# Two weight matrices of a hybrid block: seven block products for eight in 45 of 128 squares

## The chip, the cores and the metric

The kernel runs on one core of a Trainium2 chip. The time is the device time of one execution in microseconds (us); the median of three runs of the kernel before is 2197.33 us (2196.93 to 2197.67). The profile is of one more execution.

## The reference

One layer, 256 positions, width 4096, all in float32. The input is normalised and multiplied by `w_in`; the columns of the product feed an mLSTM branch (8 heads) and a sparse-attention branch (16 heads), whose outputs stand side by side in `y`. Two square matrices of 4096 by 4096 follow, and they are what the change is about:

```python
x = x + jnp.concatenate([y_ml, y_ns], axis=-1) @ w_out[layer]
x = x + jax.nn.sigmoid(x @ ple_gate[layer]) * (p[layer] @ ple_proj[layer])
```

`p` has 256 columns, `ple_proj` is 256 by 4096.

## The kernel before

Each float32 product is made of three TensorE products in a rounded format (float32r). A number a is split into a high part, which the format holds, and the rest a - high. ScalarE makes the high part of a weight block (`whi`, line 983) and VectorE the rest (`wlo`, line 984). The same is done for the activations, which lie transposed in eight chunks of 512 rows (`sh` and `sl`, four blocks of 128 rows by 256 positions each). A product is sh x whi + sl x whi + sh x wlo, so three matmuls, all into one float32 accumulator in PSUM.

The work is a list of units. A unit is 256 rows by 512 columns of a weight matrix: one transfer of 512 KB on SyncE's queue into a `raw` buffer, one `whi`, one `wlo` (both 128x1024), and 12 matmuls of 128x512: 2 blocks of rows, 2 halves of the 256 positions (t = 0, 1), 3 products each (`mm` in `wide_group`, lines 733 and 735). A group is 16 units, 512 columns by 4096 rows, and owns two PSUM banks, tag mm0 for t = 0 and mm1 for t = 1. Each tag has two buffers, so a group may begin while the group before it is evicted: `start` requires the eviction of the group before last. The other four banks (`side`) serve everything else. There are 30 groups for w_in, then o0 to o7 for w_out, then g0 to g7 for ple_gate, each of these with one more unit of ple_proj.

The order on each engine is written out by the main loop at the end (there is no scheduler). For unit n it issues the split of unit n + LOOK (LOOK is 2), the next load, what the unit requires, its matmuls, and then one step of a queue of generators, which hold the rest of the work: `urgent` first, then `fifo`. A `require(flag)` steps that queue until the flag is set. The split buffers are LOOK + 1 deep, so the copy for a unit waits until TensorE is done with the unit LOOK + 1 places ahead of it.

Three places matter for the change:

- `t_stat` transposes a finished chunk of y (or of the new x) on TensorE into two side banks and then splits it into `sh` and `sl`; transposes run one chunk ahead of the splits. It runs chunk by chunk while the last group of the stage before still uses the older chunks. For y, the chunks c4 to c7 (columns of the mLSTM) are weighted by `hnw` during the split (lines 674 and 675).
- `t_mo` evicts the last groups of w_in (mo0 to mo3) with a sigmoid on ScalarE (line 638).
- `t_x1` adds x to an evicted group of w_out (line 865). `t_out` makes sigmoid, product with ple_proj's banks and sum for a group of ple_gate; for the last group in halves of 256 columns (lines 916 to 918).

Of the kernel before, what the change touches and what calls it, by code (L numbers as in the profile page):

```python
# [37 lines left out]

LOOK = 2
XN = (16, 19, 22, 25)  # L40
RAWB = 5


@with_exitstack
def hymba_block(ctx: ExitStack, tc: tile.TileContext, a, out: bass.AP):
# [342 lines left out]
    def t_nq(flag, g):  # L388
# [265 lines left out]

    def t_stat(chunks, weighted):

        def trans(c, col0, gate, flag):
            src, o = nat[col0 // 1024], col0 % 1024
            pp = [side(2 * (c % 2) + half, [128, 2, 256]) for half in range(2)]
            for i in range(4):  # L660
                for t in range(2):
                    k = o + i * 128
                    nc.tensor.transpose(pp[i // 2][:, i % 2, t * 128:(t + 1) * 128], src[:, t, k:k + 128], idn)  # L663
            return pp

        def split(pp, c, col0, gate, flag):
            new_stat(c)
            for half in range(2):
# [185 lines left out]
    start2 = len(units)  # L854


    def load_x(n):
        held[f"x{n}"] = utile([128, 2, 512])
        nc.gpsimd.dma_start(held[f"x{n}"], a["x"][:, n * 512:(n + 1) * 512].rearrange("(t p) c -> p t c", p=128))

    def t_x1(ps, flag, n):
        if n % 2 == 0:
            nat[n // 2] = wk.tile([128, 2, 1024], F32, tag=f"nat{n // 2}", name=f"x1_{n // 2}")
        for t in range(2):
            nc.vector.tensor_add(nat[n // 2][:, t, (n % 2) * 512:(n % 2) * 512 + 512], ps[t], held[f"x{n}"][:, t])
        done.add(flag)
        if n + 2 < 8:
            load_x(n + 2)
        yield

    def p2_post(n):
        def post(ps, flag):
            add(t_x1(ps, flag, n))
            ch = [(c, c * 512, f"p2_{c}", f"r{c}") for c in range(8)]
            if n == 6:
                add(t_stat(ch[:7], ()))
            if n == 7:
                add(t_stat(ch[7:], ()))
        return post

    for n in range(8):
        wide_group(f"o{n}", a["w_out"][n], "y" if n == 0 else None, p2_post(n), marks="p2_" if n == 7 else None)


    pbox = {}

    def proj_unit(n):
        def mm(hi, lo):
            ps = [side(2 * (n % 2) + t, [128, 512]) for t in range(2)]
            ph, pl = held["ph"], held["pl"]  # L890
            for t in range(2):
                tk = slice(t * 128, (t + 1) * 128)
                for j in range(2):
                    MM(ps[t], ph[:, j, tk], hi[:, j, :], start=(j == 0), stop=False)  # L894
                    MM(ps[t], pl[:, j, tk], hi[:, j, :], start=False, stop=False)  # L895
                    MM(ps[t], ph[:, j, tk], lo[:, j, :], start=False, stop=(j == 1))  # L896
            pbox[n] = ps
        gemm_unit(a["ple_proj"][n], mm, (lambda: require("r7")) if n == 0 else None)
# [12 lines left out]
    def t_out(ps, flag, n):
        u = utile([128, 2, 512])
        if n == 7:
            for t in range(2):
                for c in (slice(0, 256), slice(256, 512)):
                    nc.scalar.activation(u[:, t, c], ps[t][:, c], AF.Sigmoid)
                    nc.vector.tensor_tensor(u[:, t, c], u[:, t, c], pbox[n][t][:, c], op=OP.mult)
                    nc.vector.tensor_add(u[:, t, c], u[:, t, c], nat[3][:, t, 512 + c.start:512 + c.stop])
                nc.sync.dma_start(out[t * 128:(t + 1) * 128, n * 512:(n + 1) * 512], u[:, t])
            done.add(flag)  # L920
# [5 lines left out]
        for t in range(2):
            nc.vector.tensor_tensor(u[:, t], u[:, t], pbox[n][t], op=OP.mult)
            nc.vector.tensor_add(u[:, t], u[:, t], nat[n // 2][:, t, (n % 2) * 512:(n % 2) * 512 + 512])  # L928
            nc.gpsimd.dma_start(out[t * 128:(t + 1) * 128, n * 512:(n + 1) * 512], u[:, t])  # L929
# [9 lines left out]
    def load(n):  # L939
# [11 lines left out]
        if n in XN:  # L951
            j = XN.index(n)
            nat[j] = wk.tile([128, 2, 1024], F32, tag=f"nat{j}", name=f"xn{j}")
            nc.sync.dma_start(nat[j], a["x"][:, j * 1024:(j + 1) * 1024].rearrange("(t p) c -> p t c", p=128))

    def split(n):
        r = raws.pop(n)
        if n == 0:
            hi = wk.tile([128, 2, 512], F32R, tag="whi", name="whi", bufs=LOOK + 1)
            lo = wk.tile([128, 2, 512], F32R, tag="wlo", name="wlo", bufs=LOOK + 1)  # L960
# [4 lines left out]
            splits[n] = (hi, lo)  # L965
            return
        if n < 16:
            split_x(2 * n)
            split_x(2 * n + 1)
        if n - 1 in XN:  # L970
            done.add(f"xn{XN.index(n - 1)}")
        if units[n]["kind"] == "raw":
            splits[n] = (r, None)
            return
        if units[n]["kind"] == "narrow":
# [4 lines left out]
            return  # L980
        hi = wk.tile([128, 2, 512], F32R, tag="whi", name="whi", bufs=LOOK + 1)
        lo = wk.tile([128, 2, 512], F32R, tag="wlo", name="wlo", bufs=LOOK + 1)
        nc.scalar.activation(hi, r, AF.Copy)  # L983
        nc.vector.tensor_sub(lo, r, hi)  # L984
        splits[n] = (hi, lo)

    N = len(units)
    nload = 0
    while nload < RAWB:
        load(nload)  # L990
        nload += 1
# [54 lines left out]

def _layout(i):
# [48 lines left out]
```

## Time and profile before

| | |
|---|---|
| median of three runs | 2197.33 us |
| the profiled execution's own time | 2197.16 us |
| its span | 2195.4 us |
| TensorE busy | 2187.1 us, 10020 matmuls |
| VectorE busy | 1154.6 us, 53% |
| ScalarE busy | 994.0 us, 45% |
| whi and wlo | 743 each, mean 1060 and 1225 ns |
| matmuls of lines 733 and 735 | 3 x 2940 |
| moved by DMA | 422.02 MB, mean 192 GB/s |

The span is the time from the first to the last instruction. A busy TensorE says that a matmul was in flight; since matmuls are pipelined, its pace is read from the starts in a timeline. In the timeline, "x2" means that two neighbouring instructions are merged in one row, and the bracket is the time that the engine stood idle ahead of it and what ended that.

### The profile page before, as it was taken

Reading aid. Unit: us, or ns where it says so; the run is one execution under the profiler, and the core shown is the slowest. Engines: PE = TensorE matmul, PEld = TensorE weight load, DVE = VectorE, ACT = ScalarE, POOL = GpSimd, SP = SyncE. Lnnn points to the kernel's source line nnn. Section 1 sums busy time; section 2 is a strip of 40 time slices with the busy share of each in tenths; the row PEclk is TensorE's granted clock in tenths of the full one; section 3 lists DMA queues with packets and bytes.
Section 4 is the critical chain, followed back from the end, with each engine's and each line's share of the span. In section 5 each row is a group of like instructions: output and inputs, shape, how many; then the busy total and the mean of one; then the engine's idle time right before and its main releaser. Section 6 shows DMA issues by size and latency. Waiting matters only on the chain.

```text
span 2195.4 us, 26113 instructions
## 1 busy us (share of the span) xinstructions
PE 2187.1 (100%) x10020; PEld 1798.6 (82%) x10020; DVE 1154.6 (53%) x1361; ACT 994.0 (45%) x1235; POOL 38.3 (2%) x82
## 2 busy tenths in 40 slices
PE   9999999999999999999999999999999999999998
PEld 7876888888888888888888888888888888888887
DVE  6553554555556555744564455564444455544444
ACT  6543444454545454444444345453333344444443
POOL 1000000000000000000000000000000000000000
PEclk9999999999999999999999999999999999999999
DMA  9667665555555464565566665656666656666664
GB/s 353 207 200 258 191 192 181 182 165 162 169 165 170 152 181 150 181 195 188 176 192 194 195 188 172 215 180 204 202 212 202 194 178 183 210 207 204 202 202 134
DMA packets 118124, 422.02 MB, mean 192 GB/s; under 512 B 13794, under 2 KB 13850, under 8 KB 118000
## 3 DMA queue, kind: packets, MB, share of 16 engines
q1 hardware_dynamic: 113840, 408.47, 58.7%
q0 software_dynamic: 4016, 11.88, 1.9%
q8 instruction: 78, 1.28, 0.2%
q14 instruction: 46, 0.38, 0.0%
q10 hardware_dynamic: 144, 0.02, 0.0%
HBM read 416.08 MB, written 4.23 MB: 191 GB/s over the span
## 4 chain that ended last, share of the span: by engine, by line
PE 100%; DVE 0%; ACT 0%; ACTq 0%; issue 0%
PE mm L733 61%; PE mm L735 30%; PE sd L508 1%; PE sd L843 1%; PE sd L663 1%; PE sd L504 1%; PE sd L495 0%; PE sd L203 0%; PE sd L894 0%; PE sd L895 0%; PE sd L896 0%; PE sd L418 0%; PE sd L462 0%; PE sd L461 0%; PE sd L460 0%; PE sd L90 0%
## 5 line engine op out<-in xcount | busy, mean ns | idle before, releaser
L984 DVE TENSOR_TENSOR wlo<-raw,whi 128x1024 fp32r<-128x1024 f32 x743 | 910.0, 1225 | 978.3 <-ACT whi L983 973.1
L983 ACT ACTIVATE whi<-raw 128x1024 fp32r<-128x1024 f32 x743 | 787.5, 1060 | 1095.7 <-PE mm L733 988.5
L733 PE MATMUL mm<-whi,sh 128*128 128x512 f32 x2940 | 918.2, 393 | 0.0
L733 PE MATMUL mm<-whi,sl 128*128 128x512 f32 x2940 | 906.8, 390 | 0.0
L735 PE MATMUL mm<-wlo,sh 128*128 128x512 f32 x2940 | 905.7, 389 | 0.0
L733 PEld LDWEIGHTS mm<-whi,sl 128*128 128x128 f32 x2940 | 551.8, 188 | 116.6
L735 PEld LDWEIGHTS mm<-wlo,sh 128*128 128x128 f32 x2940 | 551.8, 188 | 116.2
L733 PEld LDWEIGHTS mm<-whi,sh 128*128 128x128 f32 x2940 | 543.3, 188 | 112.8 <-issue 6.7
L508 PE MATMUL sd<-vsw,pt 128*128 128x128 f32 x192 | 29.9, 292 | 0.0
L478 ACT ACTIVATE s<-s,mx 128x128 f32<-128x128 f32 (+1 forms) x64 | 28.2, 442 | 0.4 <-DVE mx L473 0.4
L508 PEld LDWEIGHTS sd<-vsw,pt 128*128 128x128 f32 x192 | 23.8, 190 | 3.9
L488 ACT ACTIVATE s<-s,sm 128x128 f32<-128x128 f32 (+1 forms) x64 | 25.2, 440 | 0.4 <-DVE sm L484 0.3
L547 DVE SCALAR_TENSOR_TENSOR sq<-u,convw_c,sq 128x256 f32<-128x256 f32 x48 | 23.3, 485 | 1.7
L152 ACT ACTIVATE u<-mm,rt 128x512 f32<-128x512 f32 x12 | 8.3, 689 | 25.4 <-PE mm L735 25.4
L473 DVE TENSOR_REDUCE mx<-s 128x2 f32<-128x256 f32 (+1 forms) x32 | 17.7, 553 | 1.1
L471 DVE TENSOR_TENSOR s<-sd,tb 128x256 f32<-128x256 f32 (+1 forms) x32 | 17.7, 553 | 0.0
L500 DVE COPY pt<-sd 128x256 f32<-128x256 f32 (+1 forms) x32 | 17.6, 550 | 0.0
L843 PE MATMUL sd<-raw,xq 128*60 128x256 f32 x128 | 17.3, 391 | 0.0
L154 DVE TENSOR_SCALAR u<-mm,rt 128x512 f32<-128x512 f32 x12 | 9.0, 751 | 14.5 <-PE mm L735 14.5
L407 POOL DMA_DIRECT2D tb<-rext_d x16 | 8.6, 540 | 458.2 <-DVE s L471 426.1
L495 PEld LDWEIGHTS sd<-idn,s 128*128 128x128 f32 x96 | 12.4, 140 | 4.2
L929 POOL DMA_DIRECT2D out_x<-u x14 | 7.6, 546 | 460.2 <-DVE u L928 460.2
(223 smaller groups left out, 710.7 us busy)
## 6 DMA issues: line engine op xcount, KB each, us to landing
raw<-in_w_in SPq DMA_DIRECT2D x479, 512.0 KB, 3.6
raw<-in_w_out SPq DMA_DIRECT2D x128, 512.0 KB, 3.5
raw<-in_ple_gate SPq DMA_DIRECT2D x128, 512.0 KB, 3.7
raw<-in_w SPq DMA_DIRECT2D x16, 512.0 KB, 3.5
u<-in_xt SPq DMA_DIRECT2D x16, 256.0 KB, 7.6
xn<-in_x SPq DMA_DIRECT2D x4, 1024.0 KB, 6.2
u<-in_x POOLq DMA_DIRECT2D x8, 512.0 KB, 4.9
raw<-in_ple_proj SPq DMA_DIRECT2D x8, 512.0 KB, 3.7
```

Of the source, the lines that this page charges most:

```text
L471: nc.vector.tensor_tensor(sb[i], psd[i], bias[:, None, :].to_broadcast([128, 2, n]), op=OP.add)
L478: nc.scalar.activation(sb[i][:, b], sb[i][:, b], AF.Exp, bias=mx[i][:, b:b + 1], accum_out=sums[i][:, b:b + 1])
L488: nc.scalar.activation(sb[i][:, b], sb[i][:, b], AF.Copy, scale=sums[i][:, b:b + 1])
L504: MM(o[t][:, h, :], pct[32 * h:32 * h + NCMP, t, :], vcmp[32 * h:32 * h + NCMP, g, :], start=True, stop=False)
L508: MM(o[t][:, h, :], ptb[i][:, b, s, :], v[:, s, b, g * 128:(g + 1) * 128], start=False, stop=(b == 1 and s == t))
L547: nc.vector.scalar_tensor_tensor(acc[:, h], c[:, h, i:i + 256], w[:, i:i + 1], acc[:, h], op0=OP.mult, op1=OP.add)
L663: nc.tensor.transpose(pp[i // 2][:, i % 2, t * 128:(t + 1) * 128], src[:, t, k:k + 128], idn)
L733: MM(box["ps"][t], s[c][:, k, t * 128:(t + 1) * 128], m[:, j, :], start=st, stop=False)
L735: MM(box["ps"][t], sh[c][:, k, t * 128:(t + 1) * 128], lo[:, j, :], start=False, stop=last)
L843: MM(o[64 * kv:64 * kv + 60], xq[l // 8][:, l % 8, 60 * kv:60 * kv + 60], raw[:, j, 256 * kv:256 * kv + 256], start=(l == 0), stop=(l == 31))
L983: nc.scalar.activation(hi, r, AF.Copy)
L984: nc.vector.tensor_sub(lo, r, hi)
```

## The change

w_out and ple_gate are now worked in eight groups of 1024 columns (0 to 3 are w_out, 4 to 7 ple_gate), in squares: 256 rows by 1024 columns, with the 256 positions, are two by two by two blocks. kp counts the 16 squares of a group. A whole square ("C") is two units of 12 matmuls. A mixed square is computed with seven block products in place of eight (Winograd's form of Strassen's scheme), so 21 matmuls: the weight blocks and the activation blocks are summed first, and the products land in seven accumulators, from which the four results are summed again. A group has four accumulators of its own results (`own[t][j]`, j the half of the columns) and, where it mixes squares, four others (`oth`, which hold three products and one more shared by results); the two sets of four banks change roles from group to group (`bank`).

A mixed square stands in two parts around a whole one: "a", two units with loads (3 and 6 matmuls), then the whole square, then "c", two units without loads (6 and 6), whose weights are sums of the four raw blocks of "a". `PLANS` gives each group's squares.

```diff
-LOOK = 2
+LOOK = 3
-RAWB = 5
+RAWB = 6
+MIXED = (3, 5, 7, 9, 11, 13)
+def _plan(head, mixed, between, tail):
+    p = [("C", k) for k in head]
+    for m, k in zip(mixed, between):
+        p += [("a", m), ("C", k), ("c", m)]
+    return p + [("C", k) for k in tail]
+PROJ = [("p", 0), ("p", 1)]
+PLANS = [
+    _plan((0, 1, 2, 3), (5, 7, 9, 11, 13), (4, 6, 8, 10, 12), (14, 15)),
...
+] + [_plan((0,), (), (), ()) + PROJ + _plan((1,), MIXED, (2, 4, 6, 8, 10, 12), (14, 15))] * 3
...
+    def bank(bset, i, shape):
+        if bset:
+            return side(i, shape)
+        return psp.tile(shape, F32, tag=f"mm{i // 2}", name=f"mm{i // 2}", bufs=2)
```

Group 1 and 2 mix six squares behind two whole ones, group 3 six behind one, group 4 four behind five whole ones and the two units of ple_proj: 5 + 6 + 6 + 6 + 4 + 3 x 6 = 45. `t_stat` makes the summed activation blocks `cb` of a mixed square behind the split:

```diff
+                kp = 2 * c + half
+                if kp in MIXED:
+                    f = stile([128, 4, 128])
...
+                            nc.scalar.activation(f[:, 2 * i:2 * i + 2].rearrange("p a t -> p (a t)"), p[:, i], AF.Copy,
+                                                 scale=hnw[:, k:k + 1])
...
+                    nc.vector.tensor_sub(f[:, 3:0:-2], f[:, 1::-1], f[:, 3:0:-2])
+                    nc.vector.tensor_sub(f[:, 0], f[:, 0], f[:, 3])
+                    nc.vector.tensor_sub(f[:, 2], f[:, 2], f[:, 0])
+                    cb[kp] = mixed_tiles(kp)
+                    nc.scalar.activation(cb[kp][0], f, AF.Copy)
+                    nc.vector.tensor_sub(cb[kp][1], f, cb[kp][0])
```

The units of a mixed square, and what a group requires when it starts:

```diff
+        def start():
+            require("ev_mo2" if g == 0 else f"oth{g - 1}")
+            if g == 0:
+                require("ev_mo3")
+            if g == 4:
+                require("r1")
+            for i, (t, j) in enumerate(((0, 0), (1, 0), (0, 1), (1, 1))):
+                own[t][j].t = bank(bset, i, [128, 512])
...
+            def split2(r):
+                r0 = raw[kp][0]
+                raw[kp].append(r)
+                hl = split_all(r, keep=True)
+
+                nc.vector.tensor_add(r0[:, 1], r0[:, 1], r0[:, 0])
+                nc.vector.tensor_add(r0[:, 0], r0[:, 0], r[:, 0])
+                nc.vector.tensor_add(r[:, 0], r[:, 0], r0[:, 1])
+                nc.vector.tensor_add(r[:, 1], r[:, 1], r[:, 0])
+                return hl
+            def mm1(hi, lo):
+                emit(product(oth[0], blocks(kp)(0, 0), hi[:, 0], lo[:, 0]))
+            def mm2(hi, lo):
+                emit(product(own[0][0], mixed(kp, 2), hi[:, 0], lo[:, 0]))
+                emit(product(own[0][1], blocks(kp)(1, 0), hi[:, 1], lo[:, 1]))
+            unit(w[kp, 0], split1, mm1, kp, True)
+            unit(w[kp, 1], split2, mm2, kp)
...
+            unit(None, lambda _: split_all(raw[kp][0]), mm1)
+            unit(None, lambda _: split_all(raw[kp][1]), mm2, post=post)
```

`t_x1_oth` and `t_out_oth` sum the four `oth` banks into the group's x or into its two output tiles, `t_x1_own` and `t_out_own` then add the `own` banks. In the last group the latter works in halves of 256 columns, one after the other:

```diff
+        if g == 7:
+            for j in range(2):
+                for t in range(2):
+                    for c in (slice(0, 256), slice(256, 512)):
+                        w = us[j][:, t, c]
+                        nc.vector.tensor_add(w, own[t][j].t[:, c], w)
+                        nc.scalar.activation(w, w, AF.Sigmoid)
+                        nc.vector.tensor_tensor(w, w, pj[:, j, t, c], op=OP.mult)
+                        nc.vector.tensor_add(w, w, x1[:, t, 512 - 512 * j + c.start:512 - 512 * j + c.stop])
+                    nc.sync.dma_start(out[t * 128:(t + 1) * 128, 3584 - 512 * j:4096 - 512 * j], us[j][:, t])
```

Besides, a load is issued as soon as fewer than six raw tiles are held, x is loaded 1024 columns at a time, the products of ple_proj are copied out of their banks, the product of the compressed branch stands last among the accumulations of an attention head, and the scratch for software-made descriptors is 4096 bytes.

On VectorE, in the middle of the w_out stage, the list was nothing but wlo, with the additions of x (line 865) at the end of each group:

```order
L865 TENSOR_TENSOR x_0_11356<-mm_11038,u 128x512
L865 TENSOR_TENSOR x_0_11356<-mm_11039,u 128x512
L984 TENSOR_TENSOR wlo<-raw,whi 128x1024 x16
L865 TENSOR_TENSOR x_0_11356<-mm_11367,u 128x512
L865 TENSOR_TENSOR x_0_11356<-mm_11368,u 128x512
```

Now a pattern of a, whole square and c reads so (line 1243 is wlo of the first unit of a, line 1236 every other wlo, lines 1105 to 1108 the sums of raw weights):

```order
L1243 TENSOR_TENSOR wlo<-raw,whi 128x512
L1236 TENSOR_TENSOR wlo<-raw,whi 128x1024
L1105 TENSOR_TENSOR raw<-raw 128x512
L1106 TENSOR_TENSOR raw<-raw 128x512
L1107 TENSOR_TENSOR raw<-raw 128x512
L1108 TENSOR_TENSOR raw<-raw 128x512
L1236 TENSOR_TENSOR wlo<-raw,whi 128x1024 x4
```

The four sums stand between the wlo of a's second unit and the wlo of the whole square's first; the four wlo at the end are the whole square's two and c's two.

On ScalarE, at the end of w_in's last group mo3 (its banks are mm_10617 and mm_10618 before, mm_10625 and mm_10626 now), before:

```order
L983 ACTIVATE whi<-raw 128x1024 x2
L674 ACTIVATE sh_10973<-sd_10907,hnw_c 128x256 x2
L674 ACTIVATE sh_10973<-sd_10908,hnw_c 128x256 x2
L983 ACTIVATE whi<-raw 128x1024
L674 ACTIVATE sh_11001<-sd_10963,hnw_c 128x256 x2
L674 ACTIVATE sh_11001<-sd_10964,hnw_c 128x256 x2
L983 ACTIVATE whi<-raw 128x1024
L638 ACTIVATE u<-mm_10617,rt 128x512
L638 ACTIVATE u<-mm_10618,rt 128x512
```

and now:

```order
L724 ACTIVATE sh_11014<-sd_10939,hnw_c 128x256 x2
L724 ACTIVATE sh_11014<-sd_10940,hnw_c 128x256 x2
L738 ACTIVATE s<-sd_10940,hnw_c 128x256 x2
L746 ACTIVATE cb<-s 128x512
L1235 ACTIVATE whi<-raw 128x1024
L724 ACTIVATE sh_11050<-sd_11004,hnw_c 128x256 x2
L724 ACTIVATE sh_11050<-sd_11005,hnw_c 128x256 x2
L738 ACTIVATE s<-sd_11005,hnw_c 128x256 x2
L746 ACTIVATE cb<-s 128x512
L1235 ACTIVATE whi<-raw 128x1024
L673 ACTIVATE u<-mm_10625,rt 128x512
L673 ACTIVATE u<-mm_10626,rt 128x512
```

Each of the chunks shown (c5 and c6) has three more ScalarE instructions, lines 738 and 746, and line 746 waits for VectorE's differences; the sigmoids of mo3 keep their place behind them. Group o0 took mo2's two banks at its start; group 0 takes both buffers of mm0 and of mm1, so mo3's too.

On VectorE at the end of the program, before (lines 917 and 918 are product and sum):

```order
L917 TENSOR_TENSOR u<-u,sd_15931 128x256
L918 TENSOR_TENSOR u<-u,x_3_13123 128x256
L917 TENSOR_TENSOR u<-u,sd_15931 128x256
L918 TENSOR_TENSOR u<-u,x_3_13123 128x256
L917 TENSOR_TENSOR u<-u,sd_15932 128x256
```

and now (line 996 adds a bank to the piece; ScalarE's sigmoid, line 997, lies between 996 and 998):

```order
L996 TENSOR_TENSOR u<-sd_15998,u 128x256
L998 TENSOR_TENSOR u<-u,pj 128x256
L999 TENSOR_TENSOR u<-u,x_3_13167 128x256
L996 TENSOR_TENSOR u<-sd_15999,u 128x256
L998 TENSOR_TENSOR u<-u,pj 128x256
L999 TENSOR_TENSOR u<-u,x_3_13167 128x256
```

There were four pieces of two instructions; there are eight of three, and the sigmoid now waits for VectorE and VectorE for the sigmoid within each piece.

## Rows read from the trace of the kernel before

**Rows 1.** The page: engines' busy time, and the chain that ended last, by engine.

```profile
PE 2187.1 (100%) x10020; PEld 1798.6 (82%) x10020; DVE 1154.6 (53%) x1361; ACT 994.0 (45%) x1235; POOL 38.3 (2%) x82
...
PE 100%; DVE 0%; ACT 0%; ACTq 0%; issue 0%
```

**Rows 2.** Timeline of TensorE, last group: start us, length us, engine, line, operation.

```profile
2177.44 0.61 PE L733 MATMUL mm<-whi,sh 128*128 128x512 f32 x2
...
2180.16 0.61 PE L733 MATMUL mm<-whi,sh 128*128 128x512 f32 x2
...
2186.96 0.39 PE L722 MATMUL mm<-whi,sh 128*128 128x512 f32 x1
...
2189.45 0.39 PE L722 MATMUL mm<-wlo,sh 128*128 128x512 f32 x1
```

**Rows 3.** Windows, w_out stage: busy us per engine, granted clock, DMA share, GB/s.

```profile
1500.00:1600.00 100.00, 100.00 (x443) 82.81 (x442) 48.63 (x43) 38.96 (x37) 2.17 (x3) 1.00 0.65 209
```

**Rows 4.** Timeline of all engines, one unit in the last group.

```profile
2175.83 1.06 ACT L983 ACTIVATE whi<-raw 128x1024 fp32r<-128x1024 f32 x1 [1.66 <-PE mm L733]
...
2176.08 0.61 PE L733 MATMUL mm<-whi,sh 128*128 128x512 f32 x2
...
2176.92 1.23 DVE L984 TENSOR_TENSOR wlo<-raw,whi 128x1024 fp32r<-128x1024 f32 x1 [1.49 <-ACT whi L983]
```

**Rows 5.** Timeline of VectorE in the ple_gate stage.

```profile
1913.56 1.23 DVE L984 TENSOR_TENSOR wlo<-raw,whi 128x1024 fp32r<-128x1024 f32 x1 [2.69 <-ACT whi L983]
1914.70 0.68 DVE L927 TENSOR_TENSOR u<-u,sd 128x512 f32<-128x512 f32 x1
1915.42 0.69 DVE L928 TENSOR_TENSOR u<-u,x 128x512 f32<-128x512 f32 x1
1916.03 1.22 DVE L984 TENSOR_TENSOR wlo<-raw,whi 128x1024 fp32r<-128x1024 f32 x1
```

**Rows 6.** Groups by form: count, then busy us, mean ns, idle us ahead.

```profile
L680 DVE TENSOR_TENSOR sl<-sd,sh 128x512 fp32r<-128x512 f32 x24 | 15.3, 681 | 0.0
...
L918 DVE TENSOR_TENSOR u<-u,x 128x256 f32<-128x256 f32 x4 | 1.7, 425 | 0.1
...
L964 DVE TENSOR_TENSOR wlo<-raw,whi 128x512 fp32r<-128x512 f32 x2 | 1.4, 692 | 1.4 <-ACT whi L963 1.4
...
L963 ACT ACTIVATE whi<-raw 128x512 fp32r<-128x512 f32 x2 | 1.3, 630 | 1.3 <-DMA raw<-in_w_in 1.3
...
L488 ACT ACTIVATE s<-s,sm 128x256 f32<-128x256 f32 x32 | 14.3, 494 | 0.1
...
L679 ACT ACTIVATE sh<-sd 128x512 fp32r<-128x512 f32 x24 | 12.8, 585 | 0.0
```

**Rows 7.** Timeline of ScalarE around the start of group o0.

```profile
1451.13 0.48 ACT L674 ACTIVATE sh<-sd,hnw_c 128x256 fp32r<-128x256 f32 x1 [0.58 <-DVE sl L675]
...
1451.50 1.05 ACT L983 ACTIVATE whi<-raw 128x1024 fp32r<-128x1024 f32 x1
...
1453.35 1.06 ACT L983 ACTIVATE whi<-raw 128x1024 fp32r<-128x1024 f32 x1 [0.79 <-ACT whi L983]
...
1463.36 1.26 ACT L638 ACTIVATE u<-mm,rt 128x512 f32<-128x512 f32 x2
```

**Rows 8.** Timeline of TensorE, last transposes ahead of group o0.

```profile
1456.28 1.03 PE L663 MATMUL sd<-idn,y 128*128 128x128 f32 x8
1457.07 0.71 PE L733 MATMUL mm<-whi,sh 128*128 128x512 f32 x2
```

**Rows 9.** Timeline of VectorE at the end of the program.

```profile
2189.39 0.42 DVE L918 TENSOR_TENSOR u<-u,x 128x256 f32<-128x256 f32 x1
...
2189.74 0.41 DVE L917 TENSOR_TENSOR u<-u,sd 128x256 f32<-128x256 f32 x1
...
2191.76 0.42 DVE L918 TENSOR_TENSOR u<-u,x 128x256 f32<-128x256 f32 x1
```

**Rows 10.** Windows, behind the last matmul.

```profile
2192.00:2194.00 2.00, 0.00 (x0) 0.00 (x0) 0.19 (x1) 0.00 (x0) 0.00 (x0) 0.57 0.41 159
```

More of the change, by code (lines that the diff above doesn't have):

```diff
@@ L853, in hymba_block @@
                        after=cmp_unit if name == "vw" else None)
[L854 to L898, printed above, removed]
     def t_p():
-        pr = pttile([128, 2, 256])
+        pr = utile([128, 2, 256])
         nc.gpsimd.dma_start(pr, a["p"])
         yield
-        ph = wk.tile([128, 2, 256], F32R, tag="a", name="ph")
-        pl = wk.tile([128, 2, 256], F32R, tag="b", name="pl")
+        ph, pl = (wk.tile([128, 2, 256], F32R, tag="s", name=n, bufs=3) for n in ("ph", "pl"))
         nc.scalar.activation(ph, pr, AF.Copy)
@@ L908, in t_p, with load_x @@
         held["ph"], held["pl"] = ph, pl
+        done.add("p")
         yield
-    def t_out(ps, flag, n):
-        u = utile([128, 2, 512])
-        if n == 7:
-            for t in range(2):
[L915 to L920, printed above, removed]
+    def load_x(g):
+        nat[g] = wk.tile([128, 2, 1024], F32, tag=f"nat{g}", name=f"x1_{g}")
+        nc.gpsimd.dma_start(nat[g], a["x"][:, g * 1024:(g + 1) * 1024].rearrange("(t p) c -> p t c", p=128))
@@ new lines, in t_out_own @@
+    def t_out_own(g, own, us, pj):
+        while f"mix{g}" not in done:
+            yield
+        x1 = nat[g - 4]
+        if g == 7:
+            for j in range(2):
+                for t in range(2):
[6 more added lines that the diff above has]
+                    nc.sync.dma_start(out[t * 128:(t + 1) * 128, 3584 - 512 * j:4096 - 512 * j], us[j][:, t])
+            done.add("own7")
@@ L921, in t_out @@
             return
-        for t in range(2):
-            nc.scalar.activation(u[:, t], ps[t], AF.Sigmoid)
-        done.add(flag)
+        for j in range(2):
+            for t in range(2):
+                nc.vector.tensor_add(us[j][:, t], own[t][j].t, us[j][:, t])
+        done.add(f"own{g}")
         yield
[L926 to L929, printed above, removed]
+        for j in range(2):
+            u = us[j]
+            nc.scalar.activation(u, u, AF.Sigmoid)
+            nc.vector.tensor_tensor(u, u, pj[:, j], op=OP.mult)
@@ L930, in t_out, with emit @@
             yield
-    for n in range(8):
-        wide_group(f"g{n}", a["ple_gate"][n], "r" if n == 0 else None,
-                   lambda ps, flag, n=n: add(t_out(ps, flag, n)), after=lambda u, n=n: proj_unit(n) if u == 7 else None)
+            c0 = 512 - 512 * j
+            nc.vector.tensor_add(u, u, x1[:, :, c0:c0 + 512])
+            nc.gpsimd.dma_start(out[:, (g - 4) * 1024 + c0:(g - 4) * 1024 + c0 + 512].rearrange("(t p) c -> p t c", p=128), u)
+            yield
+    def emit(seq):
+        for acc, s, m in seq:
+            MM(acc.t, s, m, start=acc.i == 0, stop=acc.i == acc.n - 1)
+            acc.i += 1
@@ L937, in hymba_block @@
+    for g in range(4):
+        pair_group(g, a["w_out"][g], "p1_")
+    for g in range(4, 8):
+        pair_group(g, a["ple_gate"][g - 4], "r")
     raws, splits = {}, {}
@@ L979, in split, with load_some @@
             splits[n] = (hl, None)
[L980 to L985, printed above, removed]
-    N = len(units)
[L988 to L991, printed above, removed]
+            held_raw[0] -= 1
+        elif units[n]["kind"] == "pair":
+            splits[n] = units[n]["split"](r)
+        else:
+            splits[n] = split_all(r)
+    N = len(units)
+    loads = deque(n for n in range(N) if units[n]["src"] is not None)
+    def load_some():
+        while loads and held_raw[0] < RAWB:
+            held_raw[0] += 1
+            load(loads.popleft())
+    load_some()
     add(t_rms())
```

251 lines of the change are left out of this document (226 added, 25 removed).

## The prediction

> **What bounds the kernel now.** I read the page's parts on busy time and on the chain of waits first: TensorE is busy for 2187.1 of 2195.4 us, and the chain that ended last is TensorE alone [rows 1]. A busy TensorE is not yet a dense one, so the timeline comes next, for the pace. The twelve matmuls of one unit (256 rows of weights by 512 columns) start at 2177.44 and those of the next at 2180.16: 2.72 us, 0.2267 us per matmul. Where the last unit's rows stand one by one, six matmuls into the same bank and then six into the other, the first starts at 2186.96 and the twelfth at 2189.45: 0.2264 each [rows 2]. So one accumulator alone runs at the same pace. VectorE is busy in 48.63 of 100 us in the w_out stage [rows 3]. In every stage it is TensorE that sets the end; only what follows the last matmul (2189.45 + 0.39 = 2189.84) is bare.
>
> What I need besides is how a unit's weights get ready. ScalarE starts the copy whi 0.25 us before the next unit's first matmul (2175.83, 2176.08), which is when TensorE is done with the high halves of the unit in whose buffer it writes; it takes 1.06 us, and VectorE's wlo starts 0.03 us behind it and takes 1.23 [rows 4]. VectorE starts an operation that needs nothing from the one ahead 0.09 us before that one ends (1913.56 + 1.23 against 1914.70; 0.61 from a 512-wide start to the next, 1915.42 to 1916.03), but one that waits for its forerunner 0.03 us after its end: 0.72 from start to start (1914.70, 1915.42) [rows 5].
>
> **What is removed.** A whole square is 24 matmuls, a mixed one 21. 45 mixed squares drop 135 matmuls of 128x512: 135 x 0.2267 = 30.6 us off TensorE. ple_proj keeps its 96. The loads are as many and as large as before, so SyncE's queue carries the same; POOL's four loads of x are twice as large and half as many, and each is issued a group ahead of its use.
>
> [...] Rows 2 show 226 to 227 ns here, with a weight load ahead of each, and the measurement decides.
>
> **What is added beside other work.** In a mixed square VectorE makes one 512-wide wlo (0.69), three 1024-wide ones and four 512-wide sums: about 0.6 + 3 x 1.14 + 2.8 = 6.8 us at starts 0.09 apart from ends, where a whole square has 2.3 to 2.5. A repeat of the pattern (mixed square a, whole square, mixed square c) is 45 matmuls, 10.2 us, with 9.2 us of VectorE. By throughput it fits; latency is another matter.
>
> **Term 1, the wait in each repeated pattern.** Put 0 at the first matmul behind the whole square's second unit C2. Units c1, c2, a1', a2' follow (6, 6, 3, 6 matmuls), so C1' starts at 21 x 0.2267 = 4.76, and its fifth matmul, the first with wlo, is due at 5.67. With four buffers, a2' writes into C2's: whi at -0.25 to 0.81, wlo at 0.84 [rows 4]; the first sum 1.14 later at 1.98; each of the other three waits for the one ahead: 2.70, 3.42, 4.14; then C1's wlo, queued behind the sums, at 4.14 + 0.61 = 4.75 to 5.98 [rows 5]. TensorE waits 0.31, with a hop 0.35 us. The first pattern of a group has none (its a2 writes into a buffer freed two units earlier): 45 - 8 = 37 waits, 13.0 us. Bounds: 0, were the sums all 0.61 apart (the chain then ends at 5.65, before it is due); 0.55 each (20 us), were every operation held to 0.72. I take 0.35, the rows' own spacing.
>
> [...]
>
> **Term 2, the start of group 0.** Its four accumulators need both buffers of both tags, so its second matmul waits for the sigmoid that evicts mo3's first bank; before, group o0 took only mo2's. On ScalarE that sigmoid stands behind whi's and the splits of chunks c4 to c6. It started at 1463.36 (two in 1.26) [rows 7]; mo3's last matmuls follow the transposes at 1456.28, 24 of them from 1457.07, so TensorE is free at 1462.5 [rows 8]. Even undelayed, the second matmul (due 1462.7) would wait to 1464.0: 1.3 us. Now each of c4, c5, c6 gets, between its fourth sh copy and the next whi (1451.13, 1451.50: nothing lies there now), two more 256-wide copies, three short differences on VectorE, the copy to cb: 0.37 + 0.48 + 0.03 + 0.43 + 2 x (0.03 + 0.29) + 0.03 + 0.63 = 2.6, less the 0.05 of a pipelined start, 2.55 [rows 6, 7] (0.29 for 128 columns is an estimate from 0.692 at 512 and 0.425 at 256). Only one slack lies in that chain, 0.79 before whi at 1453.35, of which VectorE's queue leaves 0.7. Three times 2.55 less 0.7 is 6.95; the wait is 1.3 + 6.95 = 8.2 us. Chunks c1 to c3 come out even: split, sums and two wlo's need 6.3 us of the 6.33 that TensorE gives them. Bounds 6 and 10. Behind the waiting matmul stands all of group 0; ScalarE and VectorE catch up while TensorE waits, so nothing further is late.
>
> [...]
>
> **Term 3, the start of group 4.** Chunk 1 of the new stationary is transposed into the two banks of own[0][1] and own[1][1], so the eighth matmul waits until VectorE has read them. VectorE has ahead of that the four own-adds of group 3 (the third waits for the last unit; 0.61 apart they end 1.85 us behind group 3), one wlo (to 2.97) and two sl of 0.68, to 4.2; due was 1.59 [rows 5, 6]. Wait 2.6. After that each chunk c1 to c6 with its sums holds ScalarE and VectorE for 5.2 us (two sl 1.2, differences 1.0, copy 0.63, whi 1.06, wlo 1.25), while TensorE has 2.72 + 0.79 of work per chunk [rows 2, 8]; weights are three units ahead, and the side banks run out at c6 and c7: another 2.0. Together 4.6, bounds 2 and 8.
>
> **Term 4, the end.** Before, the last pieces are sigmoid, product, sum, with the sigmoids running ahead; VectorE ends at 2191.76 + 0.42 = 2192.18, 2.3 us behind TensorE. Now a piece begins and ends on VectorE and has ScalarE in the middle: add 0.42, hop, sigmoid 0.49 (priced by the copy of that size), hop, product 0.42, sum 0.45, next add 0.35 after the last start: 1.77 per piece [rows 6, 9], and VectorE's order lets no piece overtake. Eight pieces from 0.88 us after the last unit's start end at 15.1; TensorE ends at 2.9. 12.2 instead of 2.3: 9.9 us. Bounds 9 and 11. The output transfers behind it are the same size.
>
> **Sum.** Against the profiled execution's own 2197.16 us (span 2195.4 and 1.8 around it; the median shown, 2197.33, is 0.2 above): 2197.2 - 30.6 + 13.0 + 8.2 + 2 + 4.6 + 9.9 = 2204.3. I forecast a little slower.
>
> **Rivals.**
> B, no wait in the pattern: VectorE's chain ends before 5.67 and term 1 is gone: 2191.3, faster. For it: the wait is 0.3 us, at the edge of what rows of other operations can price. Against: each of the three later sums reads or overwrites what the one ahead touched, and the only such pair in the trace is 0.72 apart.
> C, the opening wait is not there: ScalarE gets to the sigmoid in time because the chunks are split earlier. Term 2 falls to 1.3 and the clock holds: 2195.4, or 2193 with half of term 3. Against: rows 7 show the sigmoid late already.
> D, a longer chain: VectorE held to 0.72 throughout, term 1 is 20 us: 2211.7, slower. It decides from 0.2 us more per pattern.
> [...]
> That the change doesn't do what it says is out: TensorE's order holds 135 matmuls less.
>
> **How the numbers follow.** Forecast A 0.50 (own range 2199 to 2210), B 0.22, C 0.12, D 0.14, F 0.02. A measurement of this kernel tells 0.2%, 4.4 us, from no change: 2192.9 to 2201.7 is the same. A gives 0.42 slower and 0.08 same; B 0.17 faster and 0.05 same; C 0.04 faster, 0.07 same, 0.01 slower; D and F 0.16 slower. Faster 0.21, same 0.20, slower 0.59. The range takes in B and D: 2190 to 2214.
>
> **What would show it.** In the changed trace: 2.72 us per whole unit unchanged (removal); in the chain of waits, VectorE's wlo in front of a whole square's fifth matmul, 37 times some 0.3 us (term 1); an idle TensorE of about 8 us before group 0's second matmul, ended by ScalarE's sigmoid, with the clock below 1.00 behind it (term 2); two to three gaps behind group 3 (term 3); and 12 us from the last matmul to the last VectorE operation (term 4). TensorE dense through the mixed squares, or the sigmoid at most 2 us behind mo3, would make it wrong.

## The result: 1% slower, 2218.8 us

Four executions of the changed kernel have a median of 2218.82 us (2217.71 to 2219.14), those of the kernel before 2197.29 us. The ratio is 1.0097, 95% interval 1.008 to 1.0115: slower by 21.5 us. The forecast was 2204.3 us, slower by 7, with a range up to 2214; the sign was right and the size was not. One line of the page of the changed kernel, the chain that ended last by engine:

```profile
PE 88%; DVE 6%; ACT 4%; issue 1%; DMA 0%; SPq 0%; ACTq 0%; DVEq 0%
```

Before, TensorE was busy for all of the span and was the whole chain [rows 1]. Now VectorE has 6% of the chain and ScalarE 4%: for a tenth of the time it is not TensorE that sets the end. The waits of TensorE's matmuls, by what ended them (us in total, times, longest):

```profile
PE mm L1020 <- ACT u L673: 12.4, 1, 12.4
PE sd L1020 <- DVE wlo L1236: 3.9, 20, 0.2
PE mm L1020 <- DVE wlo L1236: 3.3, 17, 0.2
```

Three of the prediction's four places are waits of TensorE, and they are there: one long wait for the sigmoid `u`; 20 + 17 = 37 waits for a `wlo`, the number that was counted; and waits for `sl` at group 4 (rows below), with one that was not foreseen, for `pl`, the split operand of ple_proj. The fourth place, the tail, lies behind the last matmul. What these rows don't tell is a wait's full price: the wait of 0.37 us from start to start in the next rows stands here with 0.2. So the prices below are taken from start to start, less the 0.2267 us of a matmul that waits for nothing. With the tail they make up the difference:

| term | forecast | measured |
|---|---|---|
| 135 matmuls removed | -30.6 | -30.6 |
| 1, the repeated pattern, 37 times | 13.0 (0.35 each) | 18.5 (0.50 each) |
| 2, the wait at the start of group 0 | 8.2 | 12.5 |
| slow clock behind it | 2 | 2.6 |
| 3, group 4, up to ple_proj | 4.6 | 9.2 |
| 4, the tail | 9.9 | 9.4 |
| sum | 7.1 | 21.6 |

The profiled execution's own time is 2219.09 us, 21.9 above that of before; the table leaves 0.3 of it open.

**The repeated pattern.** Timeline of all engines for one repeat in the last group:

```profile
2156.27 1.06 ACT L1235 ACTIVATE whi<-raw 128x1024 fp32r<-128x1024 f32 x1 [2.09 <-PE sd L1020]
...
2156.53 0.61 PE L1020 MATMUL mm<-whi,cb 128*128 128x512 f32 x2
...
2158.51 0.68 DVE L1105 TENSOR_TENSOR raw<-raw 128x512 f32<-128x512 f32 x1
...
2161.29 3.49 DVE L1236 TENSOR_TENSOR wlo<-raw,whi 128x1024 fp32r<-128x1024 f32 x3
...
2161.74 0.61 PE L1020 MATMUL sd<-whi,sl 128*128 128x512 f32 x2
...
2162.56 0.30 PEld L1020 LDWEIGHTS sd<-wlo,sh 128*128 128x128 f32 x2 [0.63 <-DVE wlo L1236]
2162.56 0.73 PE L1020 MATMUL sd<-wlo,sh 128*128 128x512 f32 x2 [0.21 <-DVE wlo L1236]
...
2163.13 0.62 PE L1020 MATMUL sd<-whi,sh 128*128 128x512 f32 x2
```

Zero of the prediction is 2156.53. The copy whi starts 0.26 ahead of it, the first sum at 1.98, the `wlo` of the whole square at 4.76, ending at 5.99; forecast were -0.25, 1.98, 4.75 and 5.98. The waiting matmul starts at 2162.56, 0.82 us behind the row of two ahead of it, which is 0.37 too much. That is the forecast wait. But the row then holds two matmuls and the next starts 0.57 us on, in place of 0.45: the second matmul is 0.11 late, and the four behind it lose another 0.02. The load of its weights is the row that is marked as waiting for `wlo`, too: nothing was loaded ahead during the wait.

**The start of group 0.** ScalarE before: the first copies to `sh` of the chunks c1 and c4.

```profile
1428.93 1.07 ACT L679 ACTIVATE sh<-sd 128x512 fp32r<-128x512 f32 x2
...
1447.93 0.45 ACT L674 ACTIVATE sh<-sd,hnw_c 128x256 fp32r<-128x256 f32 x1
```

ScalarE now: the same two copies, in c2 the two steps that wait for VectorE, c4 from its fourth copy to `sh` on, and the sigmoid of mo3:

```profile
1429.17 1.07 ACT L729 ACTIVATE sh<-sd 128x512 fp32r<-128x512 f32 x2
...
1438.77 0.60 ACT L741 ACTIVATE s<-sd 128x512 f32<-128x512 f32 x1 [1.71 <-DVE sl L730]
1440.57 0.63 ACT L746 ACTIVATE cb<-s 128x512 fp32r<-128x512 f32 x1 [1.21 <-DVE s L744]
...
1450.02 0.46 ACT L724 ACTIVATE sh<-sd,hnw_c 128x256 fp32r<-128x256 f32 x1
...
1453.41 0.48 ACT L724 ACTIVATE sh<-sd,hnw_c 128x256 fp32r<-128x256 f32 x1 [0.57 <-DVE sl L725]
1454.44 0.84 ACT L738 ACTIVATE s<-sd,hnw_c 128x256 f32<-128x256 f32 x2 [0.55 <-DVE sl L725]
...
1457.02 2.00 ACT L1235 ACTIVATE whi<-raw 128x1024 fp32r<-128x1024 f32 x2
...
1474.89 1.25 ACT L673 ACTIVATE u<-mm,rt 128x512 f32<-128x512 f32 x2
```

and TensorE's first two rows of group 0:

```profile
1462.85 0.39 PE L1020 MATMUL mm<-whi,sh 128*128 128x512 f32 x1
1475.61 0.79 PE L1020 MATMUL mm<-whi,sh 128*128 128x512 f32 x1 [12.37 <-ACT u L673]
```

The clock behind them, two windows (busy us per engine, granted clock, DMA share, GB/s):

```profile
1475.00:1477.00 2.00, 1.39 (x3) 1.16 (x4) 1.22 (x1) 2.00 (x3) 0.00 (x0) 0.50 0.00 0
1481.00:1483.00 2.00, 2.00 (x11) 1.63 (x10) 1.17 (x1) 0.00 (x0) 0.00 (x0) 1.00 0.14 55
```

The sigmoid, at 1463.36 before [rows 7], starts at 1474.89. From c1's first copy to c4's ScalarE takes 20.85 us, where it took 19.00; from there to the sigmoid 24.87, where it took 15.43. That is 1.85 us more for c1 to c3 and 9.44 more for c4 to c6. Behind 12.5 us without a matmul the granted clock was 0.50 for some 5 us (0.53 in 1479 to 1481, 1.00 in 1481 to 1483): the next matmul starts 0.59 us behind the one that waited, and eleven more follow at 0.43 us.

**The start of group 4.** TensorE's rows that waited, and ScalarE's copies to `cb` of two chunks in a row:

```profile
1826.39 0.47 PE L1020 MATMUL mm<-whi,sh 128*128 128x512 f32 x1 [1.62 <-DVE sl L730]
1827.52 0.50 PE L1020 MATMUL mm<-whi,sh 128*128 128x512 f32 x1 [0.66 <-ACT s L741]
...
1843.92 0.66 PE L713 MATMUL sd<-idn,x 128*128 128x128 f32 x4 [0.50 <-DVE sl L730]
...
1849.79 0.66 PE L713 MATMUL sd<-idn,x 128*128 128x128 f32 x4 [1.22 <-DVE sl L730]
...
1865.01 0.50 PE L1154 MATMUL sd<-whi,pl 128*128 128x512 f32 x1 [1.44 <-DVE pl L929]
```

```profile
1840.42 0.63 ACT L746 ACTIVATE cb<-s 128x512 fp32r<-128x512 f32 x1 [1.21 <-DVE s L744]
...
1846.30 0.63 ACT L746 ACTIVATE cb<-s 128x512 fp32r<-128x512 f32 x1 [1.21 <-DVE s L744]
```

The first wait is 1.8 + 1.0, forecast 2.6. A chunk takes 5.88 us (forecast 5.2), so the side banks run out earlier, at c5: 1.6 and 2.4 us. Then ple_proj waits 1.9 us for `pl`, which is queued behind the chunks.

**The tail.** VectorE's first two pieces and its last operation, and the last matmul:

```profile
2200.51 0.42 DVE L996 TENSOR_TENSOR u<-sd,u 128x256 f32<-128x256 f32 x1 [4.48 <-PE sd L1020]
...
2202.22 0.42 DVE L996 TENSOR_TENSOR u<-sd,u 128x256 f32<-128x256 f32 x1
...
2213.85 0.42 DVE L999 TENSOR_TENSOR u<-u,x 128x256 f32<-128x256 f32 x1
```

```profile
2202.12 0.39 PE L1020 MATMUL sd<-wlo,sh 128*128 128x512 f32 x1
```

A piece takes 1.71 us (2200.51 to 2202.22), and VectorE ends at 2214.27, 11.8 us behind the last matmul's end (2202.51); forecast 1.77 and 12.2.

### The profile page after: what moved, and what is told of

Same layout as the page of the kernel before. It is cut to its first block, busy times and chain, and to the rows that moved or that the text cites. A ratio compares the mean times of both kernels' runs of the same rounds, so it can differ in the third digit from the quotient of the medians.

```text
span 2217.3 us, 26509 instructions
## 1 busy us (share of the span) xinstructions
PE 2173.1 (98%) x9885; PEld 1773.4 (80%) x9885; DVE 1399.3 (63%) x1735; ACT 1093.0 (49%) x1376; POOL 32.2 (1%) x70
## 3 DMA queue, kind: packets, MB, share of 16 engines
q8 instruction: 77, 1.26, 0.2%
## 4 chain that ended last, share of the span: by engine, by line
PE 88%; DVE 6%; ACT 4%; issue 1%; DMA 0%; SPq 0%; ACTq 0%; DVEq 0%
PE mm L800 39%; PE mm L802 19%; PE mm L1020 11%; PE sd L1020 11%; DVE wlo L1236 4%; ACT whi L1235 4%; PE sd L540 1%; PE sd L910 1%; DVE raw L1105 1%; PE sd L543 1%; PE sd L529 0%; PE sd L237 0%; DVE sl L730 0%; PE sd L452 0%; DMA raw<-in_w_in 0%
## 5 line engine op out<-in xcount | busy, mean ns | idle before, releaser
L800 PE MATMUL mm<-whi,sh 128*128 128x512 f32 x1920 | 603.7, 396 | 0.3 <-ACT whi L1235 0.3
L800 PE MATMUL mm<-whi,sl 128*128 128x512 f32 x1920 | 592.5, 390 | 0.0
L802 PE MATMUL mm<-wlo,sh 128*128 128x512 f32 x1920 | 592.0, 389 | 0.1
L802 PEld LDWEIGHTS mm<-wlo,sh 128*128 128x128 f32 x1920 | 360.4, 188 | 76.7 <-DVE wlo L1236 0.5
L800 PEld LDWEIGHTS mm<-whi,sl 128*128 128x128 f32 x1920 | 360.4, 188 | 76.4
L800 PEld LDWEIGHTS mm<-whi,sh 128*128 128x128 f32 x1920 | 352.2, 188 | 77.8 <-issue 5.5
L1020 PE MATMUL mm<-whi,sh 128*128 128x512 f32 x410 | 134.2, 395 | 14.7 <-ACT u L673 12.4
L1020 PE MATMUL mm<-wlo,sh 128*128 128x512 f32 x410 | 134.8, 397 | 3.4 <-DVE wlo L1236 3.3
L1020 PE MATMUL mm<-whi,sl 128*128 128x512 f32 x410 | 132.7, 392 | 0.0
L1020 PE MATMUL sd<-wlo,sh 128*128 128x512 f32 x389 | 128.2, 396 | 3.9 <-DVE wlo L1236 3.9
L1020 PE MATMUL sd<-whi,sh 128*128 128x512 f32 x389 | 126.1, 390 | 0.0
L1020 PE MATMUL sd<-whi,sl 128*128 128x512 f32 x389 | 125.9, 390 | 0.0
L1020 PEld LDWEIGHTS mm<-whi,sh 128*128 128x128 f32 x410 | 77.0, 189 | 32.0 <-ACT u L673 12.8
L1020 PEld LDWEIGHTS mm<-wlo,sh 128*128 128x128 f32 x410 | 76.1, 189 | 26.1 <-DVE wlo L1236 11.0
L1020 PEld LDWEIGHTS mm<-whi,sl 128*128 128x128 f32 x410 | 77.6, 189 | 16.5
L1020 PEld LDWEIGHTS sd<-whi,sl 128*128 128x128 f32 x389 | 73.0, 188 | 15.5
```

The source lines that it names most:

```text
L800: MM(box["ps"][t], s[c][:, k, t * 128:(t + 1) * 128], m[:, j, :], start=st, stop=False)
L802: MM(box["ps"][t], sh[c][:, k, t * 128:(t + 1) * 128], lo[:, j, :], start=False, stop=last)
L1020: MM(acc.t, s, m, start=acc.i == 0, stop=acc.i == acc.n - 1)
```

## Experiments

Each kernel was timed beside the kernel before, and its edit is shown shortened; its time is a median, with the ratio to the kernel before and its 95% interval in brackets.

**e1_sums_later: the sums behind the wlo that TensorE needs.**

```diff
 def split2(r): ...
     hl = split_all(r, keep=True)
-    nc.vector.tensor_add(r0[:, 1], r0[:, 1], r0[:, 0])
...
+    late_sums.append((r0, r))      # done at the end of the next unit's split
```

> Only the place of the four sums changes: they stand on VectorE behind the wlo of the whole square's first unit, not ahead of it. Theory (the wlo behind the sums is what TensorE waits for, and a wait of 0.36 us costs 0.50 with the restart behind it, 37 times): the whole 18.6 us go, 2219.1 - 18.6 = 2200.5, and every repeat of the pattern takes 10.20 us instead of 10.71. Rival 1 (the slow matmuls behind the wait have another cause): only 37 x 0.36 = 13.4 us go, 2205.7. Rival 2 (VectorE has too much work in a pattern, and the wait comes back at another unit): less than 5 us go, 2214 or more.

2200.4 us (ratio to before 1.0014, 1.0005 to 1.0023). The theory's number: 18.4 us went, the wait and the restart together. On VectorE the order is now

```profile
2141.72 1.23 DVE L1236 TENSOR_TENSOR wlo<-raw,whi 128x1024 fp32r<-128x1024 f32 x1 [0.36 <-ACT whi L1235]
2142.86 0.68 DVE L1276 TENSOR_TENSOR raw<-raw 128x512 f32<-128x512 f32 x1
```

and no wait for a wlo is left on TensorE. Work of 9.2 us in 10.2 is no obstacle to VectorE; the place of four operations was.

**e6_longer: one more operation in the chain.**

```diff
     nc.vector.tensor_add(r[:, 1], r[:, 1], r[:, 0])
+    nc.vector.tensor_tensor(r[:, 1], r[:, 1], r[:, 1], op=OP.max)
```

> One more operation of VectorE on 512 columns (a maximum of the last sum with itself, so nothing changes in value) stands at the end of the four sums, ahead of the whole square's wlo. Theory (a wait costs what the wlo is late, and 0.14 us more to start again, whatever its length): 37 x 0.73 = 27.0 us more, 2246.1, and 1.23 us per repeat over the 10.20. Rival (what is lost beyond the wait grows with it, 0.50 for 0.36): 37 x 0.73 x 1.39 = 37.5 us more, 2256.6.

2245.5 us (1.0221, 1.0207 to 1.0235), 26.7 more than the changed kernel; the theory said 27.0. TensorE at one of the waits:

```profile
2163.21 0.61 PE L1020 MATMUL sd<-whi,sl 128*128 128x512 f32 x2
2164.76 0.73 PE L1020 MATMUL sd<-wlo,sh 128*128 128x512 f32 x2 [0.93 <-DVE wlo L1237]
2165.32 0.62 PE L1020 MATMUL sd<-whi,sh 128*128 128x512 f32 x2
```

The waiting matmul starts 1.55 us behind the row of two ahead of it, so it waits 1.10, where it waited 0.37 before; the row behind it starts 0.56 on, 0.11 late as before. So in both kernels the price of this wait is its length plus 0.13 us.

**e2_cb_y and e3_cb_r: the block sums out of the splits, on VectorE.**

```diff
 def split(pp, c, ...):     # in t_stat, for the chunks of y (e2) or of the new x (e3)
-    if kp in MIXED: (f from the banks, three differences, cb)
+def t_cb(kps, st):         # behind mo3's eviction (e2), behind t_p (e3): one block a unit
+    f = sh + sl            # VectorE, then the differences and cb as before
```

> For the first stationary alone the block sums (cb) are made in group 0, out of sh + sl, by steps of their own behind the evictions of mo3, and not within the split of each chunk. Theory (the sums in the splits of chunks c1 to c6 are what makes the sigmoid late): the opening wait falls from 12.5 to 1.3 us and the slow clock behind it (2.6 us) goes: 2219.1 - 13.8 = 2205.3. Rival 1 (the sigmoid is late because it stands behind the splits of c4 to c6 at all): the wait stays at 5 us or more, 2212 or later. Rival 2: the sums, now 2.4 us of VectorE for each block, are late for group 0's mixed squares and give back 3 to 6 us: 2208 to 2211.

> The same for the second stationary alone: its block sums are made behind ple_proj's operands. Theory (the sums in the splits hold ScalarE and VectorE for 5.9 us per chunk): of the 9.2 us that TensorE waits from group 4's start to ple_proj only the first wait, for VectorE's sl, stays, 1.8 us: 2219.1 - 7.4 = 2211.7. Rival (the splits themselves are too slow for a chunk in every 3.5 us): the waits at chunks c5 and c6 stay, 4 us, and only 3 us go: 2216.

e2: 2211.4 us (1.0064, 1.0052 to 1.0077). The opening wait is 1.26 us from start to start, and the run's mean granted clock is 0.997, 0.994 in the changed kernel, so the theory of its cause stands, and the second rival, too: 5.7 us come back as waits for `wlo` in group 0. TensorE at the opening, then VectorE and TensorE at the longest of the new waits:

```profile
1464.84 0.50 PE L1051 MATMUL mm<-whi,sh 128*128 128x512 f32 x1 [1.10 <-ACT u L673]
...
1485.98 0.69 DVE L1138 TENSOR_TENSOR raw<-raw 128x512 f32<-128x512 f32 x1
...
1491.08 1.22 DVE L1269 TENSOR_TENSOR wlo<-raw,whi 128x1024 fp32r<-128x1024 f32 x1
...
1492.36 0.74 PE L1051 MATMUL mm<-wlo,sh 128*128 128x512 f32 x2 [1.83 <-DVE wlo L1269]
```

That wlo stands behind four sums of weights, one block's sum and three differences, and a cb, the first of them started at 1485.98; the matmul had been due 2 us before. e3: 2222.1 us (1.0113, 1.0099 to 1.0126), 3 us more than the changed kernel, which neither side had said. The waits at c5, c6 and `pl` are all gone (6.4 us, and 0.6 of the second wait at group 4's start), as the theory had it, but the blocks, one in every unit in the midst of group 4's mixed squares, cost about 9.3 us of new waits.

**e4_tail: pieces that overlap, and two accumulators finished early.**

```diff
-for piece: add; sigmoid; product; sum
+open_(piece 0)                       # add and sigmoid
+for piece: open_(next piece); product; sum
 # last three units of group 7
-for j: for t: product(own[t][j])      # each unit
+first own[t][0] of all three units, then own[t][1] of all three
```

> The end alone: the add of the next piece stands ahead of the product of this one, and the last three units finish the two accumulators of their first 512 columns 18 matmuls before the other two. Theory (each piece waits for ScalarE, and all eight wait for the last unit): a piece takes 1.2 us of VectorE instead of 1.70, and four of the eight lie beside the last matmuls: 5.9 us from the last matmul's end to VectorE's last operation instead of 11.8: 2219.1 - 5.9 = 2213.2. Rival (VectorE's 24 operations of 0.39 us are the bound and start no earlier): 9.4 us, 2216.7.

2211.0 us (1.0064, 1.005 to 1.0078). Its VectorE and last matmul:

```profile
2196.36 0.76 DVE L996 TENSOR_TENSOR u<-sd,u 128x256 f32<-128x256 f32 x2 [1.76 <-PE sd L1027]
...
2198.07 0.42 DVE L996 TENSOR_TENSOR u<-sd,u 128x256 f32<-128x256 f32 x1
...
2199.20 0.42 DVE L996 TENSOR_TENSOR u<-sd,u 128x256 f32<-128x256 f32 x1
...
2205.29 0.43 DVE L1005 TENSOR_TENSOR u<-u,x 128x256 f32<-128x256 f32 x1
```

```profile
2200.70 0.39 PE L1027 MATMUL sd<-wlo,sh 128*128 128x512 f32 x1
```

A piece takes 1.13 us (2198.07 to 2199.20) and the first starts 4.3 us ahead of the last matmul; VectorE ends 4.6 us behind TensorE. 7.1 of the 11.8 went, more than the 5.9 expected; the price of a piece, 1.2, was a little too high, which is part of it. The kernel gained 7.8 in all; behind the opening wait TensorE lost 1.6 us here, 2.6 in the changed kernel, and the run's mean granted clock is 0.995 and 0.994.

**e5_best and e7_cb_y_pool: the block sums on GpSimd.** As e2 (and e3), with `nc.gpsimd` for `nc.vector` in `t_cb`; e5 with the edits of e1 and e4 as well.

> The edits of e1 and e4 together, and the block sums of both stationaries made behind the splits as in e2 and e3, but on GpSimd, which is idle, in place of VectorE. Theory (four costs, each with a cause of its own, and VectorE's load is why e2 and e3 gave back): 18.6 + 13.8 + 7.4 + 8.1 = 47.9 us go, 2171.2, and no wait of TensorE for a wlo is left in groups 0 and 4. Rival 1 (GpSimd is slow at these operations and the mixed squares wait for cb): 2176 to 2190, with waits for cb in the trace. Rival 2 (the costs overlap, so they don't add): above 2190.

> e2 with the block sums of the first stationary on GpSimd. Theory (the 5.4 us that e2 gave back in group 0 were VectorE's work queued ahead of wlo's): they go, 2205.3 to 2206. Rival 1 (GpSimd slows VectorE beside it, or is too slow): the wlo's or the cb's are late and 3 us or more stay: 2208 or later.

e7: 2215.6 us (1.0085, 1.0071 to 1.0099), worse than e2; e5: 2199.0 us (1.0008, 0.9999 to 1.0018). In e7 the first rival came true. In e5 the time lies in the second rival's range, but the trace has the first one's cause: the waits that were to go are gone, some 46 us with the tail, so the costs do add, and new waits put 26 us back, 11 in group 0 and 15 in group 4, all of them for `whi` and `wlo`, not for cb itself. ScalarE and VectorE of e7 in group 0 (VectorE by operation, 1478 to 1504):

```profile
1490.30 0.63 ACT L719 ACTIVATE cb<-u 128x512 fp32r<-128x512 f32 x1 [5.25 <-POOL u L714]
```

```profile
L1269 DVE TENSOR_TENSOR wlo<-raw,whi 128x1024 fp32r<-128x1024 f32 x5 | 8.6, 1726 | 11.0 <-ACT whi L1268 11.0
L1139 DVE TENSOR_TENSOR raw<-raw 128x512 f32<-128x512 f32 x1 | 1.7, 1673 | 0.0
```

ScalarE's copy to cb waits 5.25 us for GpSimd's last difference, and the whi that TensorE needs stands behind it in ScalarE's queue. Moving work to an idle engine moved the wait to the queue of the engine between. Part of it is that both engines are slower side by side, as the last section shows; the two parts were not taken apart.

**e8_spread_pool and e9_spread_vec: the same work, spread out.** The edits of e1 and e4, and:

```diff
+def cb_plan(kp, st):       # called where a chunk is split; one block every second unit
+    cbq.append((at, sums))         # f = sh + sl and the differences: GpSimd (e8), VectorE (e9)
+    cbq.append((at + 3, pieces))   # ScalarE's copy to cb, three units later; cb's rest
```

> The edits of e1 and e4, and the block sums spread out: those of one block on GpSimd at every second unit from its chunk's split on, ScalarE's copy to cb three units (8.2 us) behind them, so that it never waits for GpSimd, whose sums took 4.2 us in e7. Theory (in e5 and e7 it was the copy to cb, queued on ScalarE ahead of whi's and waiting for GpSimd, that held TensorE): the sum holds now, 2219.1 - 18.6 - 13.8 - 7.4 - 8.1 = 2171.2; only the waits of 1.3 us at group 0, 1.8 at group 4 and 0.4 at the copies are left. Rival 1 (GpSimd beside VectorE slows it): wlo's late, 2176 or more. Rival 2 (the costs of the opening and of group 4 are not to be had without new ones): above 2185.

> The same places, with the sums on VectorE. Theory (VectorE has 2.4 us more for a block, in two units or one chunk of w_in, where it has 5.4 to 6.3 us of which 3.6 to 4.8 are taken; e2 and e3 lost by a block in every unit, not by the engine): the same as with GpSimd within 3 us, 2171 to 2174. Rival (VectorE is too full in these stretches): wlo's late as in e3, 2177 or more.

e8: 2176.0 us (0.9905, 0.9892 to 0.9919), 21 us faster than the kernel before. e9: 2179.3 us (0.9919, 0.9905 to 0.9932). Both theories were too low, e8's by 5 us and e9's by 5 to 8. In e8 these waits are left on TensorE from group 0 on:

```profile
PE mm L1043 <- ACT u L673: 2.7, 1, 2.7
PE mm L1043 <- DVE sl L760: 1.6, 1, 1.6
PE sd L743 <- DVE y L679: 1.1, 2, 0.8
```

No wlo and no cb is among them, so the rivals with late `wlo`s are not right as they were put, though both times lie in their ranges (e8's on the edge). The opening wait is 2.8 us and not 1.3, and another 1.6 us go where the transposes of the last chunk wait for `y`; in e9 the opening wait is 4.4 us, with 1.6 more lost behind it (mean granted clock in 1465 to 1490: 0.93, and 1.00 in e8). In the opening ScalarE now waits up to 2.13 us (e8) and 2.69 us (e9) for VectorE's `sl`, 1.33 before: in e8 three of VectorE's wlo's beside GpSimd take 1.75, 1.48 and 1.97 us (from 1454.45 to 1466.77; 1.22 in the changed kernel), in e9 the block sums stand in its queue. With 1.8 and 0.5 at group 4 and a tail 2.3 us longer than before, e8 comes to 2197.2 - 30.6 + 2.8 + 1.6 + 2.3 + 2.3 = 2175.6. So the removed matmuls do give their whole 0.2267 us.

## Why the prediction was wrong

The sign came from the right mechanism: the gain of 30.6 us was real (e8), and the four costs that were set against it are where they were put. Three of them were sized too low, by 14.4 us together.

- **Removal.** Right: e8's account closes, to 0.4 us, with 30.6 us for the 135 matmuls, 0.2267 us each.
- **Term 1** failed at "TensorE waits 0.31, with a hop 0.35 us", where the price stopped at the wait. The wait was 0.37, but TensorE loses 0.13 more to start again, and 37 times that is 4.8 us of the 5.5 that were missing. e6 shows the same 0.13 at a wait of 1.10 us, and e1 that it goes with the wait. VectorE's spacings, 0.71 to 0.73 behind a forerunner and 0.61 for the wlo that needs nothing, were those of the forecast. Rival D, 0.55 us for VectorE's sake, came near the size by another cause: the wlo did start 0.61 behind the last sum, 0.08 ahead of that sum's end. So this operation did not wait for the one ahead of it to end.
- **Term 2** failed at two steps. The first is "Chunks c1 to c3 come out even: split, sums and two wlo's need 6.3 us of the 6.33". They took 1.85 us more than before: ScalarE's and VectorE's times had been set side by side, but each step of the chain waits for the other engine, and ScalarE, in order, stands idle 1.5 to 1.7 us for `sl` and 1.2 us for the differences in each chunk. The second is the 2.55 us for each of c4 to c6. With the slack they were to add 6.95 and added 9.44: in c4 3.61 us (c5 3.89, c6 3.61) lie between the fourth copy to `sh` and the next `whi`, not 0.37 + 2.55 = 2.92, above all because ScalarE waits 0.55 us for VectorE's last `sl` ahead of the copies of line 738, and that wait is not in the sum. The two misses, 1.85 and 2.49, are the missing 4.3 us. e2 shows that the sums within the splits are the whole cause: without them 1.26 us are left, the 1.3 of the forecast.
- **The clock.** The 2 us that the sum has for a slow clock are the author's guess, and no run shows them: behind the wait of 12.5 us the changed kernel lost 2.6, and e1, e3, e4 and e6 behind the same wait 2.1, 2.3, 1.6 and 1.9 us.
- **Term 3** failed at "the side banks run out at c6 and c7: another 2.0". The first wait was right (2.8 for 2.6). The chunk was 5.88 us and not 5.2, for the same reason as in term 2, and the banks ran out at c5 and c6 for 4.0 us; and `pl` was not followed along its queue: it stands behind all chunks, 1.9 us, and 0.5 for a wlo next to it. e3 shows all of these to be the sums' doing, since they go with them.
- **Term 4** was right, and e4 shows why the tail was long: the order of VectorE's queue.
- The rivals B (no wait) and C (no opening wait) are out by the traces.

The range was made to hold B and D, whose 2211.7 has term 1 at its upper bound and all others as forecast. The upper bounds of all four terms together (20, 10, 8 and 11), with the 2 us for the clock, would have given 2217.6. Terms 2 and 3, at 12.5 and 9.2, lie above their own bounds of 10 and 8; they missed for one cause, chunks that were too long, so their errors added.

## What to carry to other kernels

When work is given to a helper engine, price the serial chain of one item, across the engines and with each in-order queue's idle time, and not the busy time of each; then ask what else stands in those queues. The waits of TensorE for a `wlo` cost 0.13 us each besides their length, 4.8 us over 37 of them, so with many short waits the number counts and not their sum alone. And where the work fits an engine by throughput, its place decides: the changed kernel and e9 have the same matmuls and nearly the same sums on the same engine, and are 40 us apart by where they stand.

## What the runs showed of the hardware

**TensorE's wait for a `wlo` cost 0.13 us more than it lasted**, whether it lasted 0.37 (the changed kernel) or 1.10 us (e6): the matmul behind the waiting one is 0.11 late, and the next few 0.02 in all.

**GpSimd and VectorE were slower side by side.** In the rows of e7 above five of VectorE's `wlo` take 1.73 us on average, 1.23 elsewhere, and one of the sums 1.67, 0.69 elsewhere, as GpSimd works beside it; GpSimd's own difference on 128 columns takes from 0.5 to 1.3 us there and up to 1.5 in e8. The longest of e8's opening ran beside a `wlo` of VectorE (started at 1467.43, 1.23 us):

```profile
1467.45 1.52 POOL L717 TENSOR_TENSOR s<-s 128x128 f32<-128x128 f32 x1
```

The sum of 512 columns took 1.27 us at best on GpSimd (e8) and 0.69 on VectorE (e2).

**The same wait, with the granted clock at 0.50 or at 1.00.** The first wait of group 4 is 1.78 us in the changed kernel and in e1, with another of 1.0 behind it. The granted clock 2 us on, in the changed kernel and in e1 (windows):

```profile
1828.00:1830.00 2.00, 2.00 (x15) 1.74 (x14) 1.21 (x3) 1.33 (x2) 0.00 (x0) 1.00 0.30 119
```

```profile
1818.00:1820.00 2.00, 2.00 (x5) 1.45 (x6) 1.18 (x4) 1.08 (x2) 0.00 (x0) 0.50 0.32 131
```

In e1 it was 0.50, and the matmuls there lost 1.8 us more (2.8 for 1.0); the waits behind them were shorter by about as much (none at c5, 0.9 us for `pl`), so e1's time doesn't show it. In e9 it was 0.50, too, from 1810 to 1812: behind that first wait, which is 1.78 in both, e8 lost 0.5 and e9 2.2 us, part of the 3.3 us between them. Why the clock fell in one kernel and not in the other stays open.
